# Batched experts on one core: the first transfer of x written directly into the Tile frame, the second behind it

## The chip, the cores and the metric

The kernel runs on one core of a Trainium2 chip. The metric is the device time of one launch in microseconds (us); lower is better. The kernel before takes 179.77 us, the median of three runs (179.73 to 179.83).

## What is computed

Eight experts, each a two-layer network with a ReLU between the layers. `x` is 8 x 256 x 512, `w1` is 8 x 512 x 2048, `w2` is 8 x 2048 x 512, all float32:

```python
h = np.matmul(x, w1)
h = np.maximum(h, 0)
return np.matmul(h, w2).astype(np.float32)
```

The weights are 64 MiB of float32 in HBM, x and the result 4 MiB each.

## The kernel before

**Numbers and layout.** All matmuls are in bfloat16. One expert's w1 and one expert's w2 are 2 MiB each as bfloat16, and SBUF has two buffers of each. The results of all eight experts stay in `out_sb` as float32 until they are written.

**Who moves what.** There are two DMA queues in use.

- GpSimd (POOL) issues every transfer that casts float32 to bfloat16 on the way: `x_c`, the x of experts 4 to 7 (L136), and all weights (`load_w1` at L126, `load_w2` at L131, and for the last two experts in two pieces at L133 and L134). It issues x_c, w1 of experts 0 and 1, then makes the identity matrix (L139 to L141), then issues w2 of experts 0 and 1. From there on it waits until a buffer is free: for w1 on `s_first` (ScalarE has read the last first-layer result of an expert), for w2 on `s_act` (the result of an expert is copied out). At its end it issues the store of experts 0 to 3 (L160).
- SyncE (SP) issues the x of experts 0 to 3 without a cast, as two transfers of 1 MiB, experts 0 and 1 and then experts 2 and 3 (L93), each on a semaphore of the kernel's own (`s_x`). Afterwards it passes on tokens: it waits for each weight's landing and for the buffers it concerns, and raises `t_w` for TensorE (L99 to L118). At the end it issues the stores of experts 4 to 6 (L120) and of expert 7 (L122) and waits until all has landed (L295).

**x on the chip.** In four rounds, VectorE and ScalarE each cast or copy one expert's x into `x_b` (L171), TensorE transposes it (L248), and the same two engines copy the transposes into `xe` (L187, L190). Rounds 0 and 1 use `x_f`, one SP transfer each; rounds 2 and 3 use `x_c`. TensorE does all four rounds before its first matmul.

**The experts.** TensorE then works in pairs of experts: first layer of both (L264), with VectorE and ScalarE taking halves of the result through ReLU (L213, L211), then second layer of both (L284), with copies into `out_sb` (L220). Each stage takes its `t_w` tokens before it starts.

**The frame around the start.** The launcher opens a Tile context (L321). Construction of that context places some constants on POOL and a barrier of all five engines (L310). Inside the frame the kernel has one critical section (L91), which holds the two SP transfers. Then `tc.close()` and `tc.compile()` (L94, L95) end the frame, and everything after that is written directly on the engines with the kernel's own semaphores. As built, this gives in order:

- SP: the opening barrier, a NoOp and a branch into the section, the two transfers, the section's end (a semaphore increment, a drain, a NoOp), then the frame's closing;
- all other engines: the opening barrier, two branches, then the frame's closing;
- the closing itself: a drain on SP, a barrier of all engines, on POOL a drain and a clearing of the two Tile semaphores, and a second barrier of all engines.

A barrier here is: each engine signals POOL and waits; POOL waits for the four signals and releases the four. SP's signal stands behind its two transfers in its instruction stream, so no engine passes the first closing barrier before SP has issued both. Nothing in the closing waits for a transfer to land.

Of the kernel before, what the change touches and what calls it, by code (L numbers as in the profile page):

```python
# [9 lines left out]
def kernel(  # L10
# [20 lines left out]
    G = E // 2  # L31
# [10 lines left out]
    x_r = x.rearrange("e (p m) k -> p e m k", m=MT)  # L42
# [3 lines left out]
    x_f = nc.alloc_sbuf_tensor("x_f", [P, G, MT, H], f32)  # L46
# [16 lines left out]
    s_x = [sem(f"s_x{i}") for i in range(G // 2)]  # L63
# [20 lines left out]
    sp, pool, act, dve, pe = nc.sync, nc.gpsimd, nc.scalar, nc.vector, nc.tensor  # L84
# [3 lines left out]

    with tc.tile_critical(no_gpsimd_drain=True):  # L91
        for r in range(G // 2):
            sp.dma_start(x_f[:, 2 * r:2 * r + 2], x_r[:, 2 * r:2 * r + 2]).then_inc(s_x[r], 16)  # L93
    tc.close()  # L94
    tc.compile()  # L95

    def copied(eng, n):
        eng.wait_ge(s_act, n)
        eng.wait_ge(s_dve, n)  # L99


    for e in range(0, E, 2):
        for b in range(2):

            if e < G:
                sp.wait_ge(s_xe[b], e // 2 + 1)
            elif e + b == G:
                for s in s_xe:
                    sp.wait_ge(s, G)
            sp.wait_ge(s_w1[e + b], 16).then_inc(t_w, 1)  # L110
        for b in range(2):
            if b:
                copied(sp, e + 1)
            if e + b < E - 2:
                sp.wait_ge(s_w2[e + b], 16).then_inc(t_w, 2)
            else:
                sp.wait_ge(s_w2[e + b], 16).then_inc(t_w, 1)
                sp.wait_ge(s_w2b[b], 16).then_inc(t_w, 1)  # L118
# [125 lines left out]
    with pe.Fori(0, G) as _r:  # L244
        take(t_xb, 2)
        for b in range(2):
            for j in range(KT1 * MT):
                ins = pe.transpose(pt[b][:, j], x_b[:, b, j], identity[:])  # L248
            ins.then_inc(s_tr, 1)

    with pe.Fori(0, G) as g:
        with pe.Fori(0, 2) as b:
            xs = ahead(xe, False, g * (4 * KT1 * C) + b * (2 * KT1 * C), [kt * C for kt in range(KT1)], C)
            take(t_w)
            with pe.Fori(0, NQ) as q:
                for i in range(FB):
# [6 lines left out]
                    for kt in range(KT1):  # L263
                        ins = pe.matmul(  # L264
                            ph[i // 2][:, i % 2, :],
                            ws[i % 2 * KT1 + kt],
                            xs[kt],
                            start=(kt == 0),
                            stop=(kt == KT1 - 1),
                        )  # L270
                    if i % 2:
                        ins.then_inc((s_hb, s_ha)[i // 2], 1)
        with pe.Fori(0, 2) as b:
            for kt in range(KT2):
# [8 lines left out]
                for m in range(MT):  # L283
                    ins = pe.matmul(  # L284
                        po[:, m],
                        hs[(kt - k0) * MT + m],
                        ws[kt - k0],
                        start=(kt == 0),
                        stop=(kt == KT2 - 1),
                    )  # L290
# [35 lines left out]
```

## Time and profile before

| | before |
|---|---|
| median of three runs | 179.77 us |
| the profiled execution's own time | 179.82 us |
| its span, first to last instruction | 178.5 us |
| mean granted TensorE clock | 0.943 |
| TensorE busy with matmuls | 134.7 us |
| POOL's DMA queue (q0) | 36.70 MB written |
| SP's DMA queue (q1) | 4.19 MB written |
| read from HBM, written to HBM | 71.30 MB, 4.19 MB |

The profiled execution is one launch; its time is 1.3 us longer than its span, which counts from the first to the last instruction. All positions are microseconds from the span's start. "Landing" is the moment at which the semaphore of a transfer has its last increment. The GB/s of the profile count what the DMA engines write, so a transfer that casts float32 to bfloat16 shows half of what it reads. Engine names: PE is TensorE (PEq its sequencer, PEld its weight loads), DVE VectorE, ACT ScalarE, POOL GpSimd, SP SyncE.

### The profile page before, as it was taken

The page shows a single profiled execution, that of the slowest core. Times are in us where ns is not written, and L with a number is a line of the kernel's source. Part 1 is how long each engine was busy: PE and PEld are TensorE (multiplying, and loading weights), DVE is VectorE, ACT ScalarE, POOL GpSimd, SP SyncE. Part 2 cuts the span into 40 slices and gives each one's busy share as a digit, 9 for nine tenths or more (in the row PEclk, how much of TensorE's full clock was granted, in tenths as well). Part 3 has the DMA queues.
Part 4 walks back from the last instruction along what each step waited for, and adds up shares of the span by engine and source line. Part 5 has one row for each costly group of instructions (what it writes and reads, how often), then busy time and mean ns, then how long its engine had stood idle before and what let it go on. Part 6 is the DMA issues. An engine that isn't in the chain of part 4 may idle for free. (4 is left out here: it accounts for less than half of the span.)

```text
span 178.5 us, 2367 instructions
## 1 busy us (share of the span) xinstructions
PE 134.7 (75%) x832; PEld 91.0 (51%) x832; DVE 37.1 (21%) x48; ACT 37.8 (21%) x49; POOL 12.2 (7%) x26
## 2 busy tenths in 40 slices
PE   0135299899949697899769399999499695998950
PEld 0224188786414296785333278874134694953420
DVE  0232672331010133131101033330100242311010
ACT  2464752222010122121100013230100221311010
POOL 2600000101010101001000100110200400000000
PEclk9999999999987999699999759999969999999996
DMA  3999899999989989989989999998998999999998
GB/s 159 370 235 235 187 224 235 206 206 235 220 191 235 228 184 235 235 176 235 235 180 231 235 195 217 235 220 191 235 228 184 235 235 190 203 209 229 284 422 343
DMA packets 4352, 40.90 MB, mean 229 GB/s; under 512 B 384, under 2 KB 384, under 8 KB 2176
## 3 DMA queue, kind: packets, MB, share of 16 engines
q0 software_dynamic: 3264, 36.70, 94.1%
q1 hardware_dynamic: 1088, 4.19, 5.7%
HBM read 71.30 MB, written 4.19 MB: 423 GB/s over the span
## 5 line engine op out<-in xcount | busy, mean ns | idle before, releaser
L264 PE MATMUL pt_h<-xe,w_sb 128*128 x512 | 67.9, 292 | 11.3 <-PEq L87 11.3
L264 PEld LDWEIGHTS pt_h<-xe,w_sb 128*128 x512 | 59.1, 148 | 20.7 <-issue 17.4
L284 PE MATMUL pt_o<-w_sb,ht_sb 128*128 x256 | 59.9, 395 | 9.2 <-PEq L87 9.2
L284 PEld LDWEIGHTS pt_o<-w_sb,ht_sb 128*128 x256 | 25.3, 101 | 42.4 <-issue 16.1
L213 DVE TENSOR_SCALAR ht_sb<-pt_h 128x512 bf16<-128x512 f32 x32 | 22.1, 692 | 53.1 <-PE pt_h L264 53.0
L211 ACT ACTIVATE ht_sb<-pt_h 128x512 bf16<-128x512 f32 x32 | 19.1, 597 | 58.0 <-PE pt_h L264 58.0
L248 PE MATMUL pt_tr<-identity,x_b 128*128 128x128 bf16 x64 | 7.5, 309 | 16.8 <-PEq L87 16.8
L220 DVE COPY out_sb<-pt_o 128x512 f32 x8 | 5.5, 692 | 65.9 <-PE pt_o L284 65.9
L220 ACT COPY out_sb<-pt_o 128x512 f32 x8 | 4.7, 585 | 64.1 <-PE pt_o L284 64.1
L248 PEld LDWEIGHTS pt_tr<-identity,x_b 128*128 128x128 bf16 x64 | 6.5, 143 | 17.5 <-issue 17.5
L126 POOL DMA_DIRECT2D w_sb<-in_w_dram x8 | 4.2, 534 | 73.2 <-ACTq L215 73.2
L131 POOL DMA_DIRECT2D w_sb<-in_w_dram x6 | 3.7, 623 | 34.5 <-ACT out_sb L220 34.4
L190 DVE COPY xe<-pt_tr 128x1024 bf16<-128x1024 bf16 x2 | 4.9, 2456 | 5.2 <-PE pt_tr L248 5.2
L190 ACT COPY xe<-pt_tr 128x1024 bf16<-128x1024 bf16 x2 | 4.9, 2472 | 4.1 <-PE pt_tr L248 4.1
L171 ACT CAST x_b<-x_f 128x1024 bf16<-128x1024 f32 x2 | 4.0, 1994 | 1.6 <-DMA x_f<-in_x_dram 1.6
L171 DVE CAST x_b<-x_f 128x1024 bf16<-128x1024 f32 x2 | 2.1, 1069 | 5.9 <-DMA x_f<-in_x_dram 5.9
L187 ACT COPY xe<-pt_tr 128x1024 bf16<-128x1024 bf16 x2 | 2.0, 1012 | 4.1 <-PE pt_tr L248 4.1
L187 DVE COPY xe<-pt_tr 128x1024 bf16<-128x1024 bf16 x2 | 1.4, 691 | 5.4 <-PE pt_tr L248 5.4
L133 POOL DMA_DIRECT2D w_sb<-in_w_dram x2 | 1.1, 528 | 17.6 <-ACT out_sb L220 17.6
L171 ACT COPY x_b<-x_c 128x1024 bf16<-128x1024 bf16 x2 | 2.2, 1118 | 0.0
L171 ACT ACT_TABLE_LOAD x1 | 1.3, 1283 | 3.0 <-PEq L95 3.0
L171 DVE COPY x_b<-x_c 128x1024 bf16<-128x1024 bf16 x2 | 1.4, 697 | 0.0
(9 smaller groups left out, 3.4 us busy)
## 6 DMA issues: line engine op xcount, KB each, us to landing
w_sb<-in_w_dram POOLq DMA_DIRECT2D x14, 2048.0 KB, 28.9
w_sb<-in_w_dram POOLq DMA_DIRECT2D x2, 1152.0 KB, 25.6
x_f<-in_x_dram SPq DMA_DIRECT2D x2, 1024.0 KB, 6.2
out_dram<-out_sb POOLq DMA_DIRECT2D x1, 2048.0 KB, 34.0
w_sb<-in_w_dram POOLq DMA_DIRECT2D x2, 896.0 KB, 29.4
out_dram<-out_sb SPq DMA_DIRECT2D x1, 1536.0 KB, 8.6
x_c<-in_x_dram POOLq DMA_DIRECT2D x1, 1024.0 KB, 9.7
out_dram<-out_sb SPq DMA_DIRECT2D x1, 512.0 KB, 5.7
```

The lines of the kernel that those rows point to most:

```text
L126: pool.dma_start(w1_k[:, e % 2 * KT1:(e % 2 + 1) * KT1], w1_r[e]).then_inc(s_w1[e], 16)
L131: pool.dma_start(w2_k[:, k:k + KT2], w2_r[e]).then_inc(s_w2[e], 16)
L133: pool.dma_start(w2_k[:, k:k + CUT], w2_r[e, :, :CUT]).then_inc(s_w2[e], 16)
L171: copy(x_b[:, b].rearrange("p (t m) q -> p t m q", m=MT), src.rearrange("p m (q t) -> p t m q", t=KT1),).then_inc(t_xb, 1)
L187: copy(xe[:, a * n:(a + 1) * n], pt[b][:].rearrange("p j q -> p (j q)")).then_inc(s_xe[b], 1)
L190: copy(xl[:, :, :, :, a - G].rearrange("p l j q -> p j l q"), pt[b][:].rearrange("p j (l q) -> p j l q", l=G),).then_inc(s_xe[b], 1)
L211: act.activation(dst, ph[half][:], relu).then_inc(t_h, 1)
L213: dve.tensor_relu(dst, ph[half][:]).then_inc(t_h, 1)
L220: copy(outs[b], po[:, half]).then_inc(s_copied, 1)
L248: ins = pe.transpose(pt[b][:, j], x_b[:, b, j], identity[:])
L264: ins = pe.matmul(ph[i // 2][:, i % 2, :], ws[i % 2 * KT1 + kt], xs[kt], start=(kt == 0), stop=(kt == KT1 - 1),)
L284: ins = pe.matmul(po[:, m], hs[(kt - k0) * MT + m], ws[kt - k0], start=(kt == 0), stop=(kt == KT2 - 1),)
```

## The change

The critical section goes. A helper `load_x(e, n, i)` issues the transfer of n experts' x from expert e on, on semaphore `s_x[i]`, and returns the instruction's name. The first transfer is issued with it while the frame is open, and its name is put in the set of instructions that get no Tile semaphore. The second is issued behind the closed frame, as SP's first instruction there.

```diff
-    with tc.tile_critical(no_gpsimd_drain=True):
-        for r in range(G // 2):
-            sp.dma_start(x_f[:, 2 * r:2 * r + 2], x_r[:, 2 * r:2 * r + 2]).then_inc(s_x[r], 16)
+    def load_x(e, n, i):
+        ins = sp.dma_start(x_f[:, e:e + n], x_r[:, e:e + n]).then_inc(s_x[i], 16)
+        return ins.ins.name
+
+    tc.no_tile_sem_insts.add(load_x(0, 2, 0))
     tc.close()
     tc.compile()
...
+    load_x(2, 2, 1)
     for e in range(0, E, 2):
         for b in range(2):
...
```

As built, this makes the following of the instruction streams:

- SP: the opening barrier, the first transfer, the frame's closing, the second transfer, then the tokens as before. The NoOp, the branch into the section, the section's semaphore increment, its drain and its second NoOp are gone.
- POOL: the clearing of Tile semaphores between the two closing barriers is gone, as is the drain ahead of it, since no Tile semaphore was used. The two closing barriers stay.
- Every other engine has one branch less ahead of the closing barriers. Behind the frame, POOL, ACT, DVE and PE have the same instructions in the same order.

The two transfers have the same sizes, addresses and semaphores as before.

## Prediction

> **What bounds the kernel now.** I read the page first, its DMA line and queues:
>
> ```profile
> span 178.5 us, 2367 instructions
> DMA  3999899999989989989989999998998999999998
> q0 software_dynamic: 3264, 36.70, 94.1%
> q1 hardware_dynamic: 1088, 4.19, 5.7%
> ```
>
> The 16 DMA engines are at 8 or 9 tenths in every slice but the first, and the two queues together took 99.8% of the span. So the next view is the table of stretches, cut fine at the start (columns behind the engines: TensorE clock, DMA share, GB/s written):
>
> ```profile
> 0.00:2.50 2.50, 0.00 (x0) 0.00 (x0) 0.00 (x0) 0.00 (x0) 0.20 (x4) 1.00 0.00 0
> 2.50:2.75 0.25, 0.00 (x0) 0.00 (x0) 0.00 (x0) 0.00 (x0) 0.00 (x0) 1.00 0.06 16
> 2.75:3.00 0.25, 0.00 (x0) 0.00 (x0) 0.00 (x0) 0.02 (x1) 0.00 (x0) 1.00 1.02 393
> 3.00:5.00 2.00, 0.00 (x0) 0.00 (x0) 0.00 (x0) 1.26 (x1) 1.58 (x3) 1.00 1.02 414
> 5.00:7.00 2.00, 0.00 (x0) 0.00 (x0) 1.08 (x1) 1.10 (x1) 1.63 (x4) 1.00 1.02 420
> 7.00:7.50 0.50, 0.00 (x0) 0.00 (x0) 0.00 (x0) 0.50 (x1) 0.50 (x2) 1.00 1.01 418
> ...
> 10.00:60.00 50.00, 37.80 (x237) 26.20 (x238) 13.71 (x15) 16.04 (x16) 1.58 (x3) 0.97 1.03 219
> 60.00:120.00 60.00, 49.89 (x325) 36.70 (x324) 13.14 (x19) 11.00 (x19) 3.17 (x6) 0.91 1.01 215
> 120.00:168.00 48.00, 41.11 (x238) 24.79 (x237) 7.61 (x11) 6.84 (x12) 3.38 (x6) 0.96 1.01 215
> 168.00:176.00 8.00, 4.08 (x19) 1.65 (x17) 0.69 (x1) 0.58 (x1) 0.00 (x0) 0.95 1.02 421
> ```
>
> This table carries the argument. Nothing moves until about 2.75 us; from then to 176 us the DMA share is 1, in every stretch. The kernel is one unbroken stream of bytes: its time is the moment of the first byte, plus a service time that no instruction in this diff touches, plus the landing of the last store. The GB/s tell who is served: the uncast x of SP at 414 to 420, POOL's casting transfers at 215 to 219. So the two SP transfers, 2.10 MB at 0.416 MB/us, or 5.0 us, fill 2.75 to about 7.8.
>
> The chain of what ended last, and the last issue behind it:
>
> ```profile
> 165.01 7.08 PE pt_o L284 x32
> 172.09 0.02 issue
> 172.12 0.58 ACT out_sb L220
> ```
>
> ```profile
> 168.65 0.39 SPq L120 DMA_DIRECT2D out_dram<-out_sb  x1
> 172.73 0.36 SPq L122 DMA_DIRECT2D out_dram<-out_sb  x1
> ```
>
> TensorE's last stage hangs on the last weights, which are part of the stream, and the stores go out on engines that are still full to 176. So the end, too, moves with the stream.
>
> **The start, instruction by instruction.** From the timeline, SP's own waits, and the line view of SP's issues:
>
> ```profile
> 0.95 0.95 SPq L93 DMA_DIRECT2D x_f<-in_x_dram  x2
> 2.98 1.28 ACT L171 ACT_TABLE_LOAD   x1 [2.98 <-PEq L95]
> 3.42 0.68 POOL L136 DMA_DIRECT2D x_c<-in_x_dram  x1 [2.97 <-POOLq L95]
> ...
> 9.71 1.06 DVE L171 CAST x_b<-x_f 128x1024 bf16<-128x1024 f32 x1
> ...
> 10.86 1.99 ACT L171 CAST x_b<-x_f 128x1024 bf16<-128x1024 f32 x1
> ...
> 24.07 1.27 PE L264 MATMUL pt_h<-xe,w_sb 128*128 x5
> ```
>
> ```profile
> SPq L310 <- PEq L310: 0.7, 1, 0.7
> SPq L95 <- PEq L95: 0.5, 2, 0.3
> ```
>
> ```profile
> L93 SPq DMA_DIRECT2D x_f<-in_x_dram x2: 433/446/459, 1.0 to 1.4; - x2
> ...
> DMA to landing us min/median/max: 4.9/6.2/7.4
> ```
>
> **Step 1, the first transfer: the one term that counts.** SP is released from the opening barrier at 0.7 and issues at 0.95. The 0.25 between hold a NoOp and a branch, which the change removes. Bounds: it gains nothing (0.00) or all (0.25); it can't lose, as less stands ahead of it on SP and nothing new does. How closely can an issue follow on SP? The two of L93 take 433 + 459 = 892 ns of the 0.95 that they span, so 0.06 lies between them; L122 starts 0.03 after the copy it waits for (172.12 + 0.58 = 172.70). I take 0.05, so the issue stands at 0.75 and the gain is **0.20 us**. The first byte came 2.75 - 0.95 = 1.80 after the issue; with the same transfer it should again, at 2.55.
>
> **Step 2, the second transfer, moved behind the closing.** Its queue is SP's; ahead of it now stand SP's drains and both closing barriers. The first issue ends at 0.75 + 0.45 = 1.20. Before, 2.98 - 1.90 = 1.08 passed from the end of the second issue to ACT's first work behind both barriers, with the section's end, a clearing and a drain on POOL that are gone. So it is issued between 1.20 and 2.28; I take 1.9. Its first byte could come 1.80 later, at 3.0 to 4.1. The first transfer keeps the engines busy for 1.05 MB / 0.416 = 2.5 us, until 5.05. Cost nothing, with a cover of about 1 us; past that each microsecond late is a hole in the stream, unless POOL's transfer fills it. SP's tokens stand behind this issue, but the first concerns a landing beyond 20 us.
>
> **Step 3, POOL's issues come earlier.** POOL issued x_c 3.42 - 1.90 = 1.52 after SP's second issue. Now it stands behind SP's first: 1.20 + 1.52 = 2.72 at the latest, 2.3 if the closing shrinks as I take it. That is 0.7 to 1.1 earlier, and worth nothing: before, x_c was issued at 3.42 and the rate still read 418 at 7.0 to 7.5, so it stood ready or nearly so behind SP's bytes.
>
> **Step 4, what the earlier POOL collides with.** The second x landed at 1.4 + 7.4 = 8.8; DVE's cast wanted it at 9.71, ACT's at 10.86, each behind earlier work. With POOL earlier and this transfer later, x_c can be served between its pieces. Bounds: undisturbed it lands 0.2 earlier, at 8.6. Served strictly in turns from 5.05 on, each of its 16 pieces per engine (4 KB is what one expert's x has in a row per partition, 2.5/16 = 0.16 us) would follow one of x_c's (8 KB in a row per partition, so 8 per engine, 1.05 MB / 0.215 / 8 = 0.61 us): 16 x 0.77 = 12.3, landing near 18. I take 12, since before the earlier transfer was served alone at 420 for over 2 us behind x_c's issue, so only its last pieces should be mixed. Then DVE's cast starts about 2.3 late, ACT's 1.1 late, and the first expert matmul slips from 24.07 to about 25. What hides it:
>
> ```profile
> 34.08 0.53 POOL L126 DMA_DIRECT2D w_sb<-in_w_dram  x1 [26.43 <-ACTq L215]
> ```
>
> ```profile
> L131 POOL DMA_DIRECT2D w_sb<-in_w_dram x6: 528/528/1086, 6.0 to 98.8; - x6
> ...
> DMA to landing us min/median/max: 28.9/30.6/44.8
> ```
>
> ```profile
> PE pt_h L264 <- PEq L87: 11.3, 7, 3.2
> PE pt_o L284 <- PEq L87: 9.2, 6, 2.6
> ```
>
> ```profile
> 52.08 1.26 PE L284 MATMUL pt_o<-w_sb,ht_sb 128*128 x3 [2.63 <-PEq L87]
> ```
>
> The next weights are issued at 34.08, when the eight MiB of weights issued at the start last until 51.9 (the second L131 issue, at 6.0 + 1.1 = 7.1, plus the longest landing, 44.8): the stream has 16 us in hand, less some 2 for start-up. And TensorE waits 11.3 + 9.2 = 20.5 us between stages, 2.63 of it ahead of 52.08, which take up the slip. Cost nothing; with that cover gone, one for one.
>
> The Trainium skill, page "DMA: Bandwidth & Descriptors", section on queues, rings and completion order, says that each DMA engine takes turns between the queue rows that have work, packet by packet. That speaks against the change, as it is the strict-turns bound above; this trace, with 418 GB/s until 7.5, does not show turns at once after x_c's issue. By the rule the sum stays the same, since turns alter the order of bytes and not their number.
>
> **The sum.** -0.20 + 0 + 0 + 0. The profiled execution, 179.82, becomes 179.62; it lies 0.05 above the median of the runs, so the median goes from 179.77 to **179.57 us**, 0.11% less.
>
> **The rivals.**
>
> - *Nothing.* The first byte is tied to something other than the issue, or the new first issue waits as long. For: 1.80 from issue to byte is long and I see nothing inside it. Against: no other event lies there. Time 179.77.
> - *POOL's start counts.* If the stream really began with POOL, its 0.7 to 1.1 us would come off: 178.7 to 179.1. Against: the full share from 2.75 on.
> - *The second x falls behind the weights* (slower). If x_c and the first two w1 are all served before it, it lands at 5.05 + 4.9 + 2 x 9.75 = 29.5 plus some 0.4, about 20 late by the 9.71 and 10.86 at which it is wanted. The deciding point is the 14 or so us in hand in step 4; beyond it POOL's w1 comes after the stream has run dry. Price 20 - 14 = 6, less 0.2: 185.6. For: at the end, L120's 1.57 MB landed 8.6 after issue (row below), where 3.7 of data at 421 and the 4.9 - 2.5 = 2.4 of the first x around it make 6.1, so POOL's store held it up by 2.5. Against: the second x is issued ahead of x_c.
>
> ```profile
> out_dram<-out_sb SPq DMA_DIRECT2D x1, 1536.0 KB, 8.6
> ```
>
> - *A hole behind the first x.* With that 2.5 added, the second x's first byte comes at 4.1 + 2.5 = 6.6, 1.5 behind 5.05, and the time is 179.57 + 1.5 = 181.1, if x_c isn't there either. Against: with nothing ahead there is nothing to be held up by.
> - *The frame's end waits for the transfer to land*, so the change does not do what it says. First x at 0.75 + 4.9 = 5.65, second issued some 0.7 later, its byte at 8.1: a hole of 3 us, 182.6. Against: before, the closing ended by 2.98, while the first x landed only at 0.95 + 4.9 = 5.85.
>
> **How the numbers follow.** Forecast 0.72 (its own range 179.45 to 179.72), nothing 0.10, POOL's start 0.09, second x behind the weights 0.04, hole 0.03, frame waits 0.02. A difference of 0.2%, 0.36 us, is about what a measurement of this kernel can tell from no change. Faster by more: POOL's start, and 0.02 of the forecast, 0.11. Slower by more: the last three, 0.09. Within: 0.80. The range takes in the two ends of step 1 (179.52 and 179.77) and 0.1 to 0.2 for the scatter of a new session: 179.35 to 179.85. Outside lie POOL's start and the slower three, 0.18.
>
> **What would show it.** In the profile of the changed kernel: the first L92 issue at 0.73 to 0.80, and a DMA share that starts by 2.55 to 2.6 instead of 2.75 (step 1). The second at 1.6 to 2.3, no fall of the share around 5 (step 2). POOL's x_c by 2.7 (step 3). The second x landing later than 8.8 in spite of it, near 12, the first expert matmul near 25, and both gone by the wait that ended at 52.08 in the trace of before (step 4). A span of 178.3. Wrong would be: any stretch from 3 to 176 with a share under 1, or a first byte that does not follow the first issue by 1.8.

## The result, and the profile after

The changed kernel takes 180.44 us, the median of 20 runs, against 179.82 us of the kernel before in 20 runs: a ratio of 1.0026, 95% interval 1.0013 to 1.0038. It is slower, though by little, and it scatters: its runs lie between 179.50 and 181.14, those of before between 179.70 and 180.23. Six of the 20 are at 179.8 or below, nine at 180.78 or above. The profiled execution is one of the long ones, at 180.78, with a span of 179.5.

The page of the changed kernel, the lines that answer to those of before:

```profile
span 179.5 us, 2360 instructions
DMA  4999989989998998999899899899989989999996
q0 software_dynamic: 3264, 36.70, 93.6%
q1 hardware_dynamic: 1088, 4.19, 6.0%
```

The table of stretches of the changed kernel (last three columns: TensorE clock, DMA share, GB/s written):

```profile
0.00:2.25 2.25, 0.00 (x0) 0.00 (x0) 0.00 (x0) 0.21 (x1) 0.20 (x4) 1.00 0.10 7
2.25:2.50 0.25, 0.00 (x0) 0.00 (x0) 0.00 (x0) 0.25 (x1) 0.02 (x1) 1.00 0.13 33
2.50:2.75 0.25, 0.00 (x0) 0.00 (x0) 0.00 (x0) 0.25 (x1) 0.25 (x1) 1.00 0.87 213
2.75:3.00 0.25, 0.00 (x0) 0.00 (x0) 0.00 (x0) 0.25 (x1) 0.25 (x1) 1.00 0.99 393
3.00:5.00 2.00, 0.00 (x0) 0.00 (x0) 0.00 (x0) 0.32 (x1) 1.72 (x5) 1.00 1.02 420
5.00:7.00 2.00, 0.00 (x0) 0.00 (x0) 1.08 (x1) 1.31 (x1) 1.81 (x2) 1.00 1.09 371
...
10.00:60.00 50.00, 29.47 (x210) 22.89 (x211) 14.03 (x15) 15.96 (x16) 1.29 (x3) 1.00 1.03 222
60.00:120.00 60.00, 53.73 (x346) 37.64 (x344) 12.45 (x18) 10.72 (x18) 3.46 (x7) 0.94 1.00 214
120.00:168.00 48.00, 40.77 (x242) 25.07 (x241) 8.30 (x12) 7.13 (x12) 3.38 (x6) 0.96 1.02 216
```

The first bytes do come earlier: the stretch from 2.50 to 2.75 showed 16 GB/s before and shows 213 now. After that the DMA share looks as unbroken as before, and by the share alone the kernel should be 0.2 us faster. The rate is not as before: from 5 to 7 us it is 371 GB/s, where it was 420. Part of that is x_c, a casting transfer that shows half of what it reads: its first packet begins at 6.31 now and began at 7.74 before.

The timeline of the changed kernel, its start and its first expert matmul, and the line view of SP's two transfers (the first issued at 0.74, the second at 1.96):

```profile
0.74 1.59 SPq L92 DMA_DIRECT2D x_f<-in_x_dram  x2
...
2.48 0.68 POOL L139 DMA_DIRECT2D x_c<-in_x_dram  x1 [2.03 <-POOLq L97]
...
21.41 2.00 ACT L174 CAST x_b<-x_f 128x1024 bf16<-128x1024 f32 x1 [10.64 <-DMA x_f<-in_x_dram]
21.41 1.08 DVE L174 CAST x_b<-x_f 128x1024 bf16<-128x1024 f32 x1 [11.81 <-DMA x_f<-in_x_dram]
...
34.63 9.05 PE L267 MATMUL pt_h<-xe,w_sb 128*128 x64
```

```profile
L92 SPq DMA_DIRECT2D x_f<-in_x_dram x2: 372/402/433, 0.7 to 2.0; - x2
...
DMA to landing us min/median/max: 4.9/12.2/19.4
```

The second x landed 19.4 us after its issue, at 21.4, and TensorE started its first expert 10.6 us later than before (34.63 against 24.07).

**Where the time went.** A landing is complete when the slowest of the 16 DMA engines has counted. The semaphore's single increments, which the trace holds, tell the engines apart; here for the w1 of expert 0 and of expert 7, us:

```
                         first engine   15th engine   last engine
before,  w1 of expert 0         22.58         22.82         22.84
changed, w1 of expert 0         22.52         22.71         23.75
before,  w1 of expert 7        148.52        148.76        148.78
changed, w1 of expert 7        148.43        148.66        149.71
```

Fifteen engines are 0.1 us earlier than before. One is 1.04 us behind the other fifteen, and it is still 1.06 behind in the weights that land at 165; in the last weights, at 169, it is 0.81 behind the fifteenth. The last weights, the last matmuls and the stores wait for it. That one lag is the difference between the spans, 178.5 and 179.5. The DMA packets of the trace show where it arose: one 4 KB packet of the second x, begun at 5.26, directly behind that engine's last packet of the first x, took 1.07 us, where such packets take 0.16. Two of the 16 engines around that moment, from the packet records put in line by their ends and starts (start in us; x for 4 KB of SP's x, . for the completion, C for 8 KB of POOL's x_c; the long row of dots is the time in which the packet of 5.26 stays open):

```
the engine behind:  5.10x 5.25. 5.26x ............................. 6.32x 6.62C 7.22x 7.39C
another:            5.00x 5.16. 5.16x 5.32x 5.47x 5.63x 5.79x 5.94x 6.09x 6.25x 6.41x 6.56x 6.72C 7.32x 7.49C
```

In the stretch table a waiting engine counts as busy, since its packet is open; only the GB/s give it away, and one engine of 16 is 6% of them.

### The profile page after: what moved, and what is told of

Its sections match the earlier page's. It is cut to its first block, busy times and chain, and to the rows that moved or that the text cites. A ratio compares the mean times of both kernels' runs of the same rounds, so it can differ in the third digit from the quotient of the medians.

```text
span 179.5 us, 2360 instructions
## 1 busy us (share of the span) xinstructions
PE 130.8 (73%) x832; PEld 89.3 (50%) x832; DVE 37.2 (21%) x48; ACT 37.9 (21%) x49; POOL 12.4 (7%) x26
## 5 line engine op out<-in xcount | busy, mean ns | idle before, releaser
L267 PE MATMUL pt_h<-xe,w_sb 128*128 x512 | 64.7, 283 | 8.3 <-PEq L87 8.3
L267 PEld LDWEIGHTS pt_h<-xe,w_sb 128*128 x512 | 57.4, 147 | 16.1 <-issue 14.2
L251 PE MATMUL pt_tr<-identity,x_b 128*128 128x128 bf16 x64 | 7.5, 309 | 27.4 <-PEq L87 27.4
```

Of the source, the lines that this page charges most:

```text
L267: ins = pe.matmul(ph[i // 2][:, i % 2, :], ws[i % 2 * KT1 + kt], xs[kt], start=(kt == 0), stop=(kt == KT1 - 1),)
```

## The experiments

Theories in the order in which they were held: an engine loses time when it passes from the first x to the second because the second is issued late (handover); it loses it because POOL's transfers are mixed in (mixing); TensorE's late start is not made up (TensorE); chance. After the first four runs the handover theory was split further. Each run stands beside runs of the kernel before on the same chip, whose median was 179.88 to 179.90 each time.

**1. The changed kernel again.** No edit.

> The changed kernel once more. Handover theory (one DMA engine loses about 1 us when it passes from the first x to the second, because the second is issued late) and mixing theory (it loses it because POOL's casting transfers are served between the pieces of the second x): in the executions that are slow, one of the 16 engines lands each weight about 1 us behind the other 15, and the time is 180.4 to 181.1; in the fast ones no engine is behind and the time is 179.5, the 0.2 us of the earlier first byte. TensorE theory (the second x lands 10 us late, and the late start of TensorE is not fully made up): the time goes with the first expert matmul, and weights land without a lagging engine. Chance theory: the scatter has nothing to do with the change, and this time both kernels show it alike.

Measured: 180.69 (180.36 to 180.93, 5 runs) against 179.89, ratio 1.0038 (1.0024 to 1.0051). In its trace two engines are behind, by 1.2 and 1.3 us in the first weight and by 1.0 or more in every later one. Chance falls.

**2. Both transfers in the open frame.**

```diff
     tc.no_tile_sem_insts.add(load_x(0, 2, 0))
+    tc.no_tile_sem_insts.add(load_x(2, 2, 1))
     tc.close()
...
-    load_x(2, 2, 1)
```

> Both transfers of x stand in the open frame, back to back, none behind it. First issue at 0.74, second at 1.23, POOL's x_c at about 3.0, which is 0.5 later than in the changed kernel and 0.4 earlier than before. Handover theory: the second x is ready long before the first is done, so no engine loses time: 179.55, no slow executions. Mixing theory: the last pieces of the second x still mix a little with x_c, so some slow executions stay, median 179.6 to 180.2. TensorE theory: the second x lands by 9 to 10, so 179.55. Chance theory: as the changed kernel, median about 180.4.

Measured: 179.65 (179.56 to 179.94, 11 runs) against 179.89, ratio 0.9985 (0.9976 to 0.9994). Issues at 0.74 and 1.23, x_c at 2.99, no engine behind. This version beats both kernels, by the 0.2 us of the earlier first byte.

**3. The old critical section with the first transfer alone; the second behind the frame.**

```diff
-        for r in range(G // 2):
-            sp.dma_start(x_f[:, 2 * r:2 * r + 2], x_r[:, 2 * r:2 * r + 2]).then_inc(s_x[r], 16)
+        sp.dma_start(x_f[:, 0:2], x_r[:, 0:2]).then_inc(s_x[0], 16)
...
+    sp.dma_start(x_f[:, 2:4], x_r[:, 2:4]).then_inc(s_x[1], 16)
```

> The kernel before, with the critical section kept, but only the first transfer in it; the second is issued behind the closed frame. First issue at 0.95 as before, second at about 2.4, x_c at about 2.95. No gain of the first byte. Handover theory: slow executions as in the changed kernel, 0.2 later: median 180.6, fast ones 179.8. Mixing theory: slow executions too, median 180.2 to 180.6, as x_c mixes with the second x. TensorE theory: second x late by some us, 180 to 180.6. Chance theory: 179.8 as before.

Measured: 180.39 (180.18 to 181.07, 11 runs) against 179.89, ratio 1.0031 (1.0019 to 1.0043). So the form of the frame is not it. The second is issued at 2.39, the latest of these four, and here nine engines open a packet of the second x that stays open for 0.8 to 1.1 us between 5.0 and 6.7; some of them had nothing open for 0.1 to 0.3 us before it.

**4. The changed kernel with POOL's first transfers later.** The identity is built ahead of them.

```diff
-    pool.dma_start(x_c[:], x_rows).then_inc(s_xc, 16)
-    load_w1(0)
-    load_w1(1)
     pool.memset(identity[:], 0.0).then_inc(s_id, 1)
...
     ).then_inc(s_id, 1)
+    pool.dma_start(x_c[:], x_rows).then_inc(s_xc, 16)
+    load_w1(0)
+    load_w1(1)
```

> The changed kernel, with POOL building the identity matrix ahead of its first three transfers instead of behind them, so that x_c is issued at about 3.9 instead of 2.5; SP's two issues stay where they are. Handover theory: the loss stays, as the second x is as late as in the changed kernel: median 180.4 with slow executions to 181. Mixing theory: the second x is taken in before x_c stands ready, lands at 8.6, no slow executions: 179.55. TensorE theory: the second x lands at 8.6, so 179.55 too.

Measured: 180.65 (180.56 to 181.41, 5 runs) against 179.89, ratio 1.0038 (1.0024 to 1.0051), two engines behind, by 0.6 and 1.6 us. The edit moved x_c less than planned, to 2.91. That makes it the partner of run 2: x_c at 2.91 and 2.99, the second x at 1.96 and 1.23, and 1.0 us between the times. In both, the second x was served mixed with x_c: it landed at 11.8 in run 2 and at 12.7 here, against 8.9 before. Mixing falls as the cause. So does TensorE: its first expert matmul stood at 25.9 in this run, and at 25.0 in run 2.

What the engines did in the handover, from the stretch from 5 to 6 us; in this order before, changed, run 2, run 3, run 4:

```profile
5.00:6.00 1.00, 0.00 (x0) 0.00 (x0) 0.10 (x1) 0.10 (x1) 0.66 (x3) 1.00 1.05 430
```

```profile
5.00:6.00 1.00, 0.00 (x0) 0.00 (x0) 0.31 (x1) 0.31 (x1) 0.91 (x2) 1.00 1.04 401
```

```profile
5.00:6.00 1.00, 0.00 (x0) 0.00 (x0) 0.35 (x1) 0.35 (x1) 0.69 (x2) 1.00 0.99 406
```

```profile
5.00:6.00 1.00, 0.00 (x0) 0.00 (x0) 0.00 (x0) 0.00 (x0) 0.77 (x2) 1.00 1.05 246
```

```profile
5.00:6.00 1.00, 0.00 (x0) 0.00 (x0) 0.42 (x1) 0.42 (x1) 0.71 (x2) 1.00 0.94 369
```

The share says 0.94 to 1.05 throughout, but run 3 moves 246 GB/s where before moved 430: the hole is there, filled with open packets.

**5. Both transfers behind the closed frame, back to back.**

```diff
-    tc.no_tile_sem_insts.add(load_x(0, 2, 0))
     tc.close()
...
+    load_x(0, 2, 0)
     load_x(2, 2, 1)
```

> Both transfers of x behind the closed frame, back to back. First issue at about 1.35, that is 0.4 later than before, second 0.49 after it. Gap theory (an engine loses up to 1 us at the handover when the second x follows the first on the same queue by 1.2 us instead of 0.5): no engine falls behind, no scatter, and the time is before plus 0.4: 180.2. Place theory (what is issued behind the closing barriers comes with the loss): 0.4 plus the loss, 180.8 to 181.5, scattered.

Measured: 180.30 (180.19 to 180.54, 8 runs) against 179.90, ratio 1.0022 (1.0012 to 1.0032). Issues at 1.39 and 1.88, no engine behind; the 0.4 is the later first issue. Its second x was mixed with POOL's transfers to the end, landing on all engines at 19.4 to 19.7, and that alone put none behind. So it is not the place behind the frame that costs, but the distance between the two.

**6. The second transfer from ScalarE's queue.**

```diff
-    load_x(2, 2, 1)
+    act.dma_start(x_f[:, 2:4], x_r[:, 2:4]).then_inc(s_x[1], 16)
```

> The changed kernel, but the second x is issued behind the closed frame by ScalarE on its own DMA queue instead of by SP, at about 2.0, the same gap of 1.2. Gap theory in its narrow form (the loss needs the same queue, whose ring the engines have read to its end): no loss, 179.6 and steady. Gap theory in its wide form (any transfer that follows the first x by 1.2) and place theory: as the changed kernel, 180.4 to 181.

Measured: 180.62 (180.49 to 180.83, 5 runs) against 179.90, ratio 1.0043 (1.0030 to 1.0056), six engines more than 0.5 behind the first. The narrow form, which needs the same queue, falls.

**7 and 8. The kernel before, with four and with eleven semaphore increments between its two transfers** (n = 4 and n = 11).

```diff
+    s_gap = sem("s_gap")
...
             sp.dma_start(x_f[:, 2 * r:2 * r + 2], x_r[:, 2 * r:2 * r + 2]).then_inc(s_x[r], 16)
+            if r == 0:
+                for _ in range(n):
+                    sp.sem_inc(s_gap, 1)
```

> The kernel before, with four semaphore increments on SP between its two transfers of x, inside the critical section: the gap grows from 0.49 to about 0.75, the closing and POOL come 0.25 later, nothing else moves. First byte as before. Gap theory: if the loss sets in with the gap, slightly more scatter, median 179.8 to 180.3. Place theory: 179.85 as before, since nothing stands behind the frame.

> The same with eleven increments: gap about 1.2 as in the changed kernel, still inside the critical section of the kernel before; POOL's x_c at about 4.1. Gap theory: one or more engines lose up to 1 us at the handover, median 180.4 to 180.9 with scatter, with the old frame and the old order. Place theory and mixing theory: 179.85, as before.

Measured: with four (issues at 0.95 and 1.69) 180.05 (179.68 to 180.20, 11 runs), ratio 1.0008 (0.9999 to 1.0017), not to be told from before. With eleven (0.95 and 2.09) 181.05 (179.99 to 181.89, 6 runs), ratio 1.0075 (1.0056 to 1.0093), a little more than the 180.4 to 180.9 expected. The old frame, the old order and 0.65 us more between two issues make a loss. The profiled execution of the second was its fastest, 179.99, and in its trace no engine is behind: the loss comes and goes between executions, and this run shows it by its times alone, not by an engine.

**9 and 10. Three experts' x in the first transfer and one in the second, and one and three.** The diff is that of 9; 10 has `load_x(0, 1, 0)` and `load_x(1, 3, 1)`, and its waits for `s_x` follow.

```diff
-    tc.no_tile_sem_insts.add(load_x(0, 2, 0))
+    tc.no_tile_sem_insts.add(load_x(0, 3, 0))
...
-    load_x(2, 2, 1)
+    load_x(3, 1, 1)
```

> The changed kernel with three experts' x in the first transfer and one in the second, so that the first keeps the engines at work until about 6.3 instead of 5.1; the second is issued at the same 1.96. Late theory (the second x reaches an engine 3.1 to 4.2 us after its issue, later than the 1.8 of the first, and an engine that is through with the first x earlier stands still until then): no engine stands still, 179.6 and steady. Fixed-price theory (a second transfer issued 1.2 behind the first costs some engine about 1 us at the handover, however long the first is): 180.4, scattered.

> One expert's x in the first transfer, three in the second, which is issued at 1.96: the first is through by 3.8. Late theory: all 16 engines stand still from 3.8 to between 5.1 and 6.2, the DMA share falls there, and the time is 179.6 plus 1.3 to 2.4: 180.9 to 182.0. Late theory with a lag that comes from engines at work: engines that are idle are reached in 1.8, at 3.8, and the time is 179.6 to 180.2. Fixed-price theory: 180.4, with some engines behind and most not.

Measured: three and one, 179.65 (179.51 to 179.91, 11 runs) against 179.88, ratio 0.9985 (0.9976 to 0.9994), no engine behind, although the second is issued at the very 1.96 of the changed kernel. The first x now keeps the engines at work until about 6.6, and what is issued at 1.96 is there by then. The fixed-price theory falls.

One and three: 185.56 (181.29 to 190.96, 7 runs), beyond what any of the theories gave; its three shortest executions, 181.29 to 183.20, are at a ratio of 1.0144 (1.0106 to 1.0182). The stretches of its profiled execution, one of the longest (190.51), and POOL's next weights:

```profile
2.00:3.00 1.00, 0.00 (x0) 0.00 (x0) 0.00 (x0) 1.00 (x1) 0.56 (x1) 1.00 0.85 307
3.00:4.00 1.00, 0.00 (x0) 0.00 (x0) 0.00 (x0) 0.28 (x1) 1.00 (x3) 1.00 0.62 197
4.00:5.00 1.00, 0.00 (x0) 0.00 (x0) 0.89 (x1) 0.00 (x0) 0.76 (x3) 1.00 0.70 119
5.00:6.00 1.00, 0.00 (x0) 0.00 (x0) 0.20 (x1) 0.00 (x0) 1.00 (x3) 1.00 0.99 303
...
10.00:60.00 50.00, 16.49 (x134) 14.67 (x135) 11.15 (x11) 15.10 (x12) 0.53 (x1) 1.00 0.86 190
```

```profile
59.23 0.53 POOL L129 DMA_DIRECT2D w_sb<-in_w_dram  x1 [52.84 <-ACTq L221]
```

Here the hole is open to most engines, and the share falls with the rate: 0.62 and 0.70, at 197 and 119 GB/s, between 3 and 5. The engines were through with the first x by 3.74, and the packets of the second x that stood open closed between 4.25 and 5.99. So its bytes came on these engines some 2.2 to 3.9 us after the issue at 1.92, though the engines had nothing else to do by then. And a second loss joins it, which the expectation did not have: the second x landed at 32.1, TensorE started its first expert at 50.3, POOL's next weights were issued at 59.23, and the stream had run dry at 53.9 when the last queued weight landed, so the share from 10 to 60 is 0.86. This second loss is read from one long execution; how the scatter of the seven divides between the two was not separated.

**11. All four experts' x in one transfer in the frame.** The `s_x[1]` wait becomes one for `s_x[0]`.

```diff
-    tc.no_tile_sem_insts.add(load_x(0, 2, 0))
+    tc.no_tile_sem_insts.add(load_x(0, 4, 0))
...
-    load_x(2, 2, 1)
```

> The x of all four experts in one transfer, in the open frame; no second one. There is no handover on SP's queue and the closing is as short as in the changed kernel. Late and fixed-price theory alike: 179.6 and steady, with the first cast at about 8.2 instead of 5.7, which TensorE makes up.

Measured: 179.89 (179.80 to 180.10, 11 runs) against 179.88, ratio 1.0001 (0.9993 to 1.0010). Steady, as expected, but without the gain, a miss. In its trace the engines lie 0.70 us apart in the first weight (22.38 to 23.08; 0.35 in run 2), and at the start four packets stay open for 0.6 to 0.7 us from 2.6 to 2.8 on. Run 9 has such packets too and kept its gain. Why this run did not was not tried.

**12. The second x alone.** SP issues it when the first has landed, and POOL issues x_c when the second has. This measures the lag; the time (185.47) is longer by construction.

```diff
+    sp.wait_ge(s_x[0], 16)
     load_x(2, 2, 1)
...
+    pool.wait_ge(s_x[1], 16)
     pool.dma_start(x_c[:], x_rows).then_inc(s_xc, 16)
```

> A measurement of the lag, not of the time: SP issues the second x only when the first has landed, and POOL issues x_c only when the second has landed, so the engines are idle when the second x is issued. If the lag comes from engines at work, its first byte comes 1.1 to 1.8 after the issue, as with the first x. If it belongs to the second transfer of a queue, 3.1 to 4.2 after. The time is some 8 us longer by construction.

Line view of the two issues (0.74 and 5.55), and stretches after the second:

```profile
L92 SPq DMA_DIRECT2D x_f<-in_x_dram x2: 373/404/434, 0.7 to 5.6; - x2
...
DMA to landing us min/median/max: 4.8/4.8/4.9
```

```profile
7.00:7.25 0.25, 0.00 (x0) 0.00 (x0) 0.00 (x0) 0.25 (x1) 0.00 (x0) 1.00 0.00 0
7.25:7.50 0.25, 0.00 (x0) 0.00 (x0) 0.00 (x0) 0.25 (x1) 0.00 (x0) 1.00 0.52 213
7.50:7.75 0.25, 0.00 (x0) 0.00 (x0) 0.00 (x0) 0.06 (x1) 0.00 (x0) 1.00 0.95 393
```

On idle engines the first packets of the second transfer open 1.0 to 1.2 us after its issue and stay open for 0.7 to 0.9; its bytes stream 1.8 to 1.9 us after the issue, like those of the first, and it lands after 4.8. In the changed kernel, issued at 1.96 among engines that the first x kept at work, it was there for the fifteen when they turned to it at 5.1 to 5.3, so within 3.1 to 3.3 at most, and its bytes came to the one behind at 6.32 - 0.16 = 6.16, 4.2 after.

POOL's queue shows the same. x_c's earliest packet came 3.3 to 4.3 us after its issue in all the other thirteen traces, and 1.4 after in this one, where the engines were idle. That is also why x_c did not fill the hole.

All runs side by side, by the time from the second issue to the landing of the first x on the median engine:

| kernel | second issued | first x landed | between | engines behind by over 0.5 | first expert matmul | median (spread) |
|---|---|---|---|---|---|---|
| 9: three and one | 1.96 | 7.00 | 5.0 | 0 | 27.4 | 179.65 (179.51 to 179.91) |
| before | 1.44 | 5.73 | 4.3 | 0 | 24.1 | 179.82 (179.70 to 180.23) |
| 2: both in frame | 1.23 | 5.43 | 4.2 | 0 | 25.0 | 179.65 (179.56 to 179.94) |
| 5: both behind | 1.88 | 6.02 | 4.1 | 0 | 32.9 | 180.30 (180.19 to 180.54) |
| 7: before, pause of 4 | 1.69 | 5.76 | 4.1 | 0 | 24.7 | 180.05 (179.68 to 180.20) |
| changed | 1.96 | 5.54 | 3.6 | 1 | 34.6 | 180.44 (179.50 to 181.14) |
| 8: before, pause of 11 | 2.09 | 5.55 | 3.5 | 0 | 23.9 | 181.05 (179.99 to 181.89) |
| 4: POOL later | 1.96 | 5.43 | 3.5 | 2 | 25.9 | 180.65 (180.56 to 181.41) |
| 6: second on ACT | 1.96 | 5.34 | 3.4 | 6 | 34.6 | 180.62 (180.49 to 180.83) |
| 3: section, first alone | 2.39 | 5.62 | 3.2 | 6 | 35.1 | 180.39 (180.18 to 181.07) |
| 10: one and three | 1.92 | 3.79 | 1.9 | 11 | 50.3 | 185.56 (181.29 to 190.96) |

Engines behind are counted in the one profiled execution of each kernel, in the landing of the first weight against its first engine. With 4.1 us or more between, none falls behind; with 3.6 or less, some do in every profiled execution but that of run 8, and all the medians are longer than before. The first expert matmul has no such order: run 5 starts it at 32.9 with no engine behind.

## Why the prediction was wrong

**What bounds the kernel: right, but read one engine too coarsely.** The time is the first byte plus an unbroken service. But it is the service of the slowest of 16 engines, and an engine that loses time once keeps its lag to the end. The share of the stretch table is a mean over 16 and counts an open packet as work. "The DMA share is 1, in every stretch" was as good as true after the change as well (1.00 to 1.03 from 10 us on).

**Step 1: right.** First issue at 0.74 (0.75 said), first bytes 0.2 earlier. Runs 2 and 9, in which no engine falls behind, measure 0.23 to 0.24 less than before in the medians, ratio 0.9985 each.

**Step 2: the step that failed.** The issue was placed well (1.96, said 1.9). But "its first byte could come 1.80 later, at 3.0 to 4.1", and so "a cover of about 1 us", took the lag of a transfer that meets idle engines. On engines that have the first x to serve it was longer. Where one stood still, the bytes came 3.3 to 4.3 us after the issue in the changed kernel and in runs 1, 3, 4 and 6 (one packet of run 4: 4.9). The cover was therefore nothing for the slowest engines, and the hole that step 2 had priced at nothing was paid by one or more of 16, at about 1 us. Run 12 measures the one lag, the changed kernel's packets the other; run 9 mends the loss by lengthening the first x, with the second issue where it is.

**The rival that came true had 0.03.** "A hole behind the first x" was the mechanism, and its condition held: x_c wasn't there either, its first packet coming at 6.31. It had 1.5 us for 181.1; the runs show some 1 us, in most executions. Its counter-argument, "with nothing ahead there is nothing to be held up by", was the error in plain words: the first x itself was ahead, and L120's 8.6 us had hinted at the same with POOL's store ahead. Whether the lag comes from packets that an engine has taken in beforehand or from something else, no run here shows. On the page "DMA: Bandwidth & Descriptors" of the Trainium skill, the specifications give a first-byte latency of about 0.6 us for this kind of issue. Measured here from the start of the issue, the first packets on idle engines open after 1.0 to 1.2 and the bytes stream after 1.8, and on busy engines that stood still they came after 3.3 to 4.3; the measurement decides.

**Step 3: right.** x_c at 2.48 (2.3 to 2.7 said), with no gain from it.

**Step 4: right in kind, wrong in size, and covered all the same.** The second x mixes with x_c and lands late, but at 21.4 and not at 12. Fifteen engines had it by 13.1; the last 8 us are the engine behind, which then shared its turns with POOL's 16 KB packets. The bound of 18 for strict turns was itself too low: it set one of x_c's packets against each of the 16 pieces, but x_c has 8 per engine, and the other turns go to weights, whose 16 KB packets take 1.23 us each. The rule of turns that the same page of the skill states in its section on queues, rings and completion order shows here plainly (x and C by turns in the packet lines above). TensorE's 10.6 us were made up except for the 0.9 by which the weights themselves are late, though not by 52 as step 4 had it, but by 92, where it waits for weights again:

```profile
91.73 8.75 PE L287 MATMUL pt_o<-w_sb,ht_sb 128*128 x32 [2.24 <-PEq L87]
```

```profile
PE pt_h L267 <- PEq L87: 8.3, 6, 2.0
PE pt_o L287 <- PEq L87: 6.5, 4, 2.6
```

Its waits between stages fell from 20.5 to 14.8 us, and its busy time from 134.7 to 130.8, at a mean granted clock of 0.966 against 0.943.

**The rival of the second x behind the weights** did not come here, but run 10 shows that it exists: there TensorE was 26 us late, past what was in hand, and the stream ran dry. In hand were 51.9 - 34.1 = 17.8 us by the prediction's own rows, not the 16, less 2, that it took.

## What to carry to other kernels

- When a stream of transfers bounds the kernel, the next one must be issued early enough to be taken up by engines at work, which took about twice as long here as by idle ones. Two issues back to back cost nothing here. What to count is the time from the second issue to the landing of the first transfer: 4.1 us was enough, and 3.6 was not.
- Look at the slowest engine, not at the mean share: compare the first and the last increment of a landing, and read the GB/s beside the share.
- A change that makes a kernel scatter where it did not before may have met a margin, as here. Lengthen what covers the margin, or shorten the pause, and see whether the scatter goes.

## What the runs showed of the hardware that was not expected

- The lag from issue to bytes of an SP transfer of 1 MiB was 1.8 us to idle engines. Behind another of 1 MiB it was 3.3 to 4.3 where an engine stood still, from SP's queue and from ScalarE's alike, and differed between the 16 engines and between executions. x_c's earliest packet, from POOL's queue, came after 1.4 us with the engines idle and after 3.3 to 4.3 with the engines at work.
- An engine 1 us behind after 6 us was still 1.06 us behind at 165 us: in 160 us it made up nothing.
- One transfer of 2 MiB in place of two of 1 MiB was 0.24 us slower than the two back to back (179.89 against 179.65), with the engines 0.70 us apart; the cause stays open.
